# The first four feature units of a hybrid decoder block share each k-step

## Chip, core and metric

The kernel runs on one core of one Trainium2 chip. The metric is device time in microseconds (us) of one execution of the whole program; lower is better. TensorE is called PE, VectorE DVE, ScalarE ACT, GpSimd POOL, and SyncE, which here only issues transfers, SP.

## What is computed

One decoder layer on a sequence of 512 tokens with 1024 channels, everything in float32. Cut to what matters here:

```
h    = rms_norm(x, norm_mix_g)                       # x: (1, 512, 1024)
proj = h @ w_in                                      # 1024 -> 12288 features
glu_in, q, k, v, g, gate_logits = split(proj)
a = glu_in[:, :1024] * sigmoid(glu_in[:, 1024:])     # GLU, then a depthwise conv of 31 taps, layer norm, silu
y_a = a @ w_conv_proj + b
r = retention(rotary(q), rotary(k), v)               # 4 heads, chunks of 128, norm, gate silu(g)
y_b = r @ w_ret_proj
x = x + (sigmoid(gA) * y_a + sigmoid(gB) * y_b) @ w_out
x = x + gated_conv_mlp(rms_norm(x))
return rms_norm(x)
```

## The kernel before

Activations lie with channels on the 128 partitions and the 512 tokens along the free dimension, so a tile of 128 channels is 128x512 and x is eight such tiles (`xs`, one for each step `kt` of a contraction over 1024 channels). The norm's factor of each token is not known when the first products start: x is only scaled by the channel gains (`g0`), multiplied, and the product is multiplied by the factor of its tokens (`rB`) when it is read out of PSUM.

Every float32 product is made of three float32r products. An operand is split into a high part (a cast on ACT) and a low part (original minus high, on DVE): `split_scaled` does it for x (`xg`), `split_half` for weights (`whi`, `wlo`, from the raw `wraw`). A matmul of a feature unit (128 features x 512 tokens in one PSUM bank) is then high x high, high x low, low x high for each of eight k-steps: 24 matmuls of 512 columns.

Weights come as one long stream of "halves" (128x1024, 512 KB, eight blocks of 128x128, so one half is one unit). `load_half` issues the transfer, `split_half` the two casts; `blocks` hands out the next blocks in order and through `upto` makes sure that halves up to `LOOK` = 2 ahead are emitted. Three buffers each hold `wraw`, `whi` and `wlo`.

At the start there is no work that needs less than x. The first two units (`unit_pair`) share each k-step, for which the stream's first two halves are stored interleaved; the third and fourth unit (`unit`) follow one after the other. `SumSq` squares each x tile on ACT and adds the squares on DVE; `stat` sums them over the channels with two matmuls against ones (line 238), DVE picks the result, POOL takes the power, and two small transfers turn it into `rB`. `stat`'s pair `wait` says after how many calls of `tick` (one for a unit) each of its stages is emitted.

The order of instructions on each engine is fixed when the program is built (a scheduler works from priorities; `tc.high_priority` moves some), and each engine then works strictly in its own order. The depthwise conv on DVE (line 368, 240 instructions) has a low priority and fills DVE between other work.

Of the kernel before, what the change touches and what calls it, by code (L numbers as in the profile page):

```python
# [9 lines left out]
F32 = mybir.dt.float32  # L10
F32R = mybir.dt.float32r
AF = mybir.ActivationFunctionType
ALU = mybir.AluOpType

P = 128
S = 512
D = 1024
KT = D // P
# [8 lines left out]
EPS = 1e-6  # L27
HS = 8 * P
LOOK = 2
WARM = 9  # L30
WPRIO = 100


_PC = {}
# [13 lines left out]
def hybrid_block(  # L48
# [10 lines left out]
    nc = tc.nc  # L59
    sb = ctx.enter_context(tc.tile_pool(name="sb", bufs=1))  # L60
# [4 lines left out]
    def nm(s):  # L65
        uid[0] += 1
        return f"{s}_{uid[0]}"

    def t512(tag, bufs, dt=F32):
        return sb.tile([P, S], dt, tag=tag, bufs=bufs, name=nm(tag))  # L70

    def tmp():
        return t512("t", 8)

    def bank():
        return psp.tile([P, S], F32, tag="ps", name=nm("ps"))

    def f32(ap):
        return ap.bitcast(F32)

    par = sb.tile([P, NPARAM], F32, tag="par", name="par")
# [6 lines left out]
    halves = {}  # L88
    emitted = [0]

    raws = {}

    def load_half(h):
        raw = sb.tile([P, HS], F32, tag="wraw", bufs=3, name=nm("wraw"))
        cut = (0, 2 * P, HS) if h == 0 else (0, HS)
        raws[h] = raw, [slice(u, v) for u, v in zip(cut, cut[1:])]
        for sl in raws[h][1]:
            nc.sync.dma_start(out=raw[:, sl], in_=wst[h][:, sl])

    def split_half(h):  # L100
        raw, sls = raws.pop(h)
        hi = sb.tile([P, HS], F32R, tag="whi", bufs=3, name=nm("whi"))
        lo = sb.tile([P, HS], F32R, tag="wlo", bufs=3, name=nm("wlo"))
        with tc.high_priority(offset=WPRIO if h > 1 else 0):
            for sl in sls:
                nc.scalar.copy(out=hi[:, sl], in_=raw[:, sl])  # L106
                nc.vector.tensor_tensor(out=lo[:, sl], in0=raw[:, sl], in1=f32(hi[:, sl]),  # L107
                                        op=ALU.subtract)
        halves[h] = (hi, lo)

    def upto(h):
        while emitted[0] <= min(h, NBLK - 1):
            load_half(emitted[0])
            split_half(emitted[0])
            emitted[0] += 1

    pos = [0]

    def blocks(n):
        b = pos[0]  # L120
        pos[0] += n
        h, c = divmod(b, 8)
        upto(h + LOOK)
        hi, lo = halves[h]
        sl = slice(c * P, (c + n) * P)
        return hi[:, sl], lo[:, sl]
# [3 lines left out]
    def later(n, fn):  # L130
        pending.append([n, fn])

    def tick():
        due = []
        for p in pending:
            p[0] -= 1
            if p[0] == 0:
                due.append(p)
        for p in due:
            pending.remove(p)  # L140
            p[1]()

    def unit(ps, rhs):
        last = len(rhs) - 1
        for kt, (xh, xl) in enumerate(rhs):
            wh, wl = blocks(1)
            nc.tensor.matmul(ps, lhsT=wh, rhs=xh, start=kt == 0, stop=False)  # L147
            nc.tensor.matmul(ps, lhsT=wh, rhs=xl, start=False, stop=False)  # L148
            nc.tensor.matmul(ps, lhsT=wl, rhs=xh, start=False, stop=kt == last)  # L149
        tick()  # L150
        return ps

    def unit_pair(rhs):
        pair = (bank(), bank())
        last = len(rhs) - 1
        for kt, (xh, xl) in enumerate(rhs):
            wh, wl = blocks(2)
            for i, ps in enumerate(pair):
                sl = slice(i * P, (i + 1) * P)
                nc.tensor.matmul(ps, lhsT=wh[:, sl], rhs=xh, start=kt == 0, stop=False)  # L160
                nc.tensor.matmul(ps, lhsT=wh[:, sl], rhs=xl, start=False, stop=False)
                nc.tensor.matmul(ps, lhsT=wl[:, sl], rhs=xh, start=False, stop=kt == last)
        tick()
        tick()
        return pair

    def split(src, tag, bufs):
        h = t512(tag, bufs, F32R)
# [5 lines left out]
    def split_scaled(src, g, tag, bufs):  # L174
        h = t512(tag, bufs, F32R)
        l = t512(tag, bufs, F32R)
        nc.scalar.activation(out=h, in_=src, func=AF.Copy, scale=g)
        nc.vector.scalar_tensor_tensor(
            out=l, in0=src, scalar=g, in1=f32(h), op0=ALU.mult, op1=ALU.subtract)
        return h, l  # L180
# [72 lines left out]
    def rsqrt_eps(v, eps):  # L253
        nc.vector.tensor_scalar(out=v, in0=v, scalar1=eps, scalar2=None, op0=ALU.add)
        return rsqrt(v)

    def stat(ss, n, eps, use, wait, dst):

        run = sums(ss)

        def second():
            ps = run()
            r = rsqrt_eps(pick(ps, n), eps)
            row = dram.tile([P, NCH], F32, tag="row", bufs=2, name=nm("row"))
            nc.gpsimd.dma_start(out=row, in_=r)
            b = t512(dst, 1)
            flat = row.rearrange("p c -> (p c)").rearrange("(o t) -> o t", o=1)
            nc.gpsimd.dma_start(out=b, in_=flat.broadcast_to([P, S]))
            later(wait[1], lambda: use(b, ps))

        later(wait[0], second)
# [8 lines left out]
    warm_ps = bank()  # L280
    for _ in range(WARM):
        nc.tensor.matmul(warm_ps[:, 0:P], lhsT=ones, rhs=ones, start=True, stop=True)
    xs = []
    g0 = sb.tile([P, KT], F32, tag="g0", name="g0")
    for i in range(KT):
        t = t512("x", 8)
        nc.sync.dma_start(out=t, in_=xT[i * P:(i + 1) * P, :])
        xs.append(t)
        if i == 0:
            nc.sync.dma_start(out=g0, in_=params[:, _PC["norm_mix_g"]:_PC["norm_mix_g"] + KT])  # L290
            load_half(0)
        if i == 3:
            load_half(1)
    ident = sb.tile([P, P], F32, tag="ident", name="ident")
    nc.sync.dma_start(out=ident, in_=ident_in)
    nc.sync.dma_start(out=par, in_=params)
    identr = sb.tile([P, P], F32R, tag="identr", name="identr")
    nc.gpsimd.tensor_copy(out=identr, in_=ident)
    onesr = sb.tile([P, P], F32R, tag="onesr", name="onesr")
    nc.gpsimd.tensor_copy(out=onesr, in_=ones)  # L300
    xg = []
    for i in range(KT):
        xg.append(split_scaled(xs[i], g0[:, i:i + 1], "xg", 16))
        if i in (0, 3):
            split_half(emitted[0])
            emitted[0] += 1

    class SumSq:
        def __init__(self):
# [10 lines left out]
    ss = SumSq()  # L320
# [4 lines left out]
    rB = [None]  # L325
# [11 lines left out]
    def times_r(ps):  # L337
        t = tmp()
        nc.vector.tensor_tensor(out=t, in0=ps, in1=rB[0], op=ALU.mult)  # L339
        return t  # L340
# [6 lines left out]
    def glu_units():  # L347
        return times_r(unit(bank(), xg)), times_r(unit(bank(), xg))

    def glu_first():  # L350
        ps = [*unit_pair(xg), unit(bank(), xg), unit(bank(), xg)]
        ts = [times_r(p) for p in ps]
        return ts[:2], ts[2:]

    def glu(ta, sg):
        nc.scalar.activation(out=sg, in_=sg, func=AF.Sigmoid)
# [46 lines left out]
        later(4, centre)  # L403


    def rope():
        p1 = unit(bank(), xg)
        p2 = unit(bank(), xg)
        res = []
        for u, v, op in ((p1, p2, ALU.subtract), (p2, p1, ALU.add)):  # L410
            m1 = tmp()
            m2 = tmp()
            nc.vector.tensor_tensor(out=m1, in0=u, in1=cosr, op=ALU.mult)
            nc.vector.tensor_tensor(out=m2, in0=v, in1=sinr, op=ALU.mult)
            nc.vector.tensor_tensor(out=m1, in0=m1, in1=m2, op=op)
            res.append(split(m1, "A", 16))
        return res
# [96 lines left out]
                add_into(yb[m], ps)  # L514


    stat(ss.acc, D, EPS, norm_mix, (2, 2), "rB")
    rg = None
    for h in range(H):
        ps = [glu_units() for _ in range(2)] if h else glu_first()  # L520
        for i in range(2):
            a = glu(*ps[i])
            with tc.high_priority(offset=-1200):
                conv(2 * h + i, a)
        dec = t512("dec", 1)
        nc.sync.dma_start(out=dec, in_=decay[h])
        q = rope()
        k = rope()
        if rg is not None:
            ret_proj(h - 1, rg)  # L530
        v = values()
        sc = scores(q, k, dec)
        sgs = []
        for e in range(DV // P):
            t = times_r(unit(bank(), xg))
            s_ = t512("G", 4)
            nc.scalar.activation(out=s_, in_=t, func=AF.Silu)
            sgs.append(s_)
        banks = inner(sc, v)
        rg = ret_norm(h, banks, sgs)  # L540
# [8 lines left out]
    for mp in range(KT // 2):  # L549
        sB = [gate(KT + 2 * mp + i, tmp()) for i in range(2)]  # L550
        for i in range(2):
            m = 2 * mp + i
            ps = unit(bank(), rg)
# [3 lines left out]
    for m in range(KT):  # L557
        ps = unit(bank(), cv)
        t = tmp()
# [4 lines left out]
    ss = SumSq()  # L564
    x1 = []
    x1g = []
    for m in range(KT):
        x_ = t512("x", 8)
        nc.sync.dma_start(out=x_, in_=xT[m * P:(m + 1) * P, :])
        ps = unit(bank(), mix)  # L570
# [46 lines left out]
    ss = SumSq()  # L617
# [174 lines left out]
```

## Time and profile before

| | |
|---|---|
| time of the runs (three) | 1086.47 to 1087.11 us, median 1087.07 |
| the profiled execution | 1086.47 us, of which span 1084.7 us |
| PE busy | 1073.2 us (99% of the span), 4834 matmuls |
| DVE / ACT / POOL busy | 71% / 39% / 2% |
| granted TensorE clock | 0.998 of full speed on average |
| read from HBM | 104.41 MB, 98 GB/s over the span |

The span runs from the first to the last instruction; 1.8 us lie around it. A busy share says how long an engine worked, not whether anything waited for it; the waits and the chain of work tell that.

### The profile page before, as it was taken

Reading aid. Unit: us, or ns where it says so; the run is one execution under the profiler, and the core shown is the slowest. Engines: PE = TensorE matmul, PEld = TensorE weight load, DVE = VectorE, ACT = ScalarE, POOL = GpSimd, SP = SyncE. Lnnn points to the kernel's source line nnn. Section 1 sums busy time; section 2 is a strip of 40 time slices with the busy share of each in tenths; the row PEclk is TensorE's granted clock in tenths of the full one; section 3 lists DMA queues with packets and bytes.
Section 4 is the critical chain, followed back from the end, with each engine's and each line's share of the span. In section 5 each row is a group of like instructions: output and inputs, shape, how many; then the busy total and the mean of one; then the engine's idle time right before and its main releaser. Section 6 shows DMA issues by size and latency. Waiting matters only on the chain.

```text
span 1084.7 us, 12428 instructions
## 1 busy us (share of the span) xinstructions
PE 1073.2 (99%) x4834; PEld 883.2 (81%) x4834; DVE 770.0 (71%) x1126; ACT 418.3 (39%) x556; POOL 24.8 (2%) x88
## 2 busy tenths in 40 slices
PE   8999999999999999999999999999999999999996
PEld 6888888888888888888888888888888888888886
DVE  7899899758996699948764555677676236767433
ACT  6334332533234331535542234444443113444331
POOL 1000000000000000000000000000000000000000
PEclk9999999999999999999999999999999999999999
DMA  7223232323322232222323532332222223222212
GB/s 274 91 98 105 68 99 95 107 68 98 98 97 88 72 110 99 81 78 88 107 98 107 146 117 98 88 113 85 94 97 97 97 98 98 90 86 97 98 58 79
DMA packets 33259, 107.33 MB, mean 99 GB/s; under 512 B 3952, under 2 KB 6256, under 8 KB 33200
## 3 DMA queue, kind: packets, MB, share of 16 engines
q1 hardware_dynamic: 32416, 104.69, 29.1%
q0 software_dynamic: 784, 1.85, 1.0%
q8 instruction: 38, 0.62, 0.2%
q14 instruction: 21, 0.17, 0.1%
HBM read 104.41 MB, written 2.11 MB: 98 GB/s over the span
## 4 chain that ended last, share of the span: by engine, by line
PE 97%; issue 1%; DVE 1%; DMA 0%; SPq 0%; POOLq 0%; ACT 0%; POOL 0%; DVEq 0%
PE ps L147 28%; PE ps L149 28%; PE ps L148 28%; PE ps L427 3%; PE ps L426 3%; PE ps L428 3%; PE ps L484 1%; PE ps L485 1%; PE ps L483 1%; PE ps L460 0%; PE ps L462 0%; PE ps L458 0%; DVE ss L183 0%; DMA x<-in_xT_dram 0%; PE ps L238 0%
## 5 line engine op out<-in xcount | busy, mean ns | idle before, releaser
L106 ACT CAST whi<-wraw 128x1024 fp32r<-128x1024 f32 (+1 forms) x185 | 193.2, 1045 | 356.5 <-PE ps L148 258.3
L107 DVE TENSOR_TENSOR wlo<-wraw,whi 128x1024 fp32r<-128x1024 f32 (+1 forms) x185 | 224.7, 1215 | 62.1 <-ACT whi L106 61.9
L147 PE MATMUL ps<-xg,whi 128*128 128x512 f32 x672 | 262.1, 390 | 0.0
L148 PE MATMUL ps<-xg,whi 128*128 128x512 f32 x672 | 261.7, 389 | 0.0
L149 PE MATMUL ps<-xg,wlo 128*128 128x512 f32 x672 | 261.5, 389 | 0.0
L149 PE MATMUL ps<-A,wlo 128*128 128x512 f32 x448 | 176.5, 394 | 0.0
L147 PE MATMUL ps<-A,whi 128*128 128x512 f32 x448 | 176.5, 394 | 0.0
L368 DVE SCALAR_TENSOR_TENSOR C<-ap,par,C 128x512 f32<-128x512 f32 x240 | 166.4, 744 | 2.9 <-ACT C L365 2.6
L148 PE MATMUL ps<-A,whi 128*128 128x512 f32 x384 | 151.3, 394 | 0.0
L149 PEld LDWEIGHTS ps<-xg,wlo 128*128 128x128 f32 x672 | 126.2, 188 | 26.5
L147 PEld LDWEIGHTS ps<-xg,whi 128*128 128x128 f32 x672 | 126.2, 188 | 26.1
L148 PEld LDWEIGHTS ps<-xg,whi 128*128 128x128 f32 x672 | 126.2, 188 | 26.1
L149 PEld LDWEIGHTS ps<-A,wlo 128*128 128x128 f32 x448 | 83.8, 187 | 20.9
L147 PEld LDWEIGHTS ps<-A,whi 128*128 128x128 f32 x448 | 83.8, 187 | 20.7
L148 PEld LDWEIGHTS ps<-A,whi 128*128 128x128 f32 x384 | 71.8, 187 | 17.7
L589 DVE SCALAR_TENSOR_TENSOR t<-ap,par,t 128x512 f32<-128x512 f32 x96 | 71.7, 750 | 2.3 <-ACT t L586 0.7
L339 DVE TENSOR_TENSOR t<-ps,rB 128x512 f32<-128x512 f32 x48 | 32.5, 685 | 55.2 <-PE ps L149 55.2
L183 DVE TENSOR_TENSOR x<-x,ps 128x512 f32<-128x512 f32 (+1 forms) x50 | 33.0, 663 | 53.4 <-PE ps L149 49.9
L583 DVE TENSOR_TENSOR ap<-ps,rB 128x512 f32<-128x512 f32 x48 | 33.1, 691 | 48.4 <-PE ps L149 45.5
L147 PE MATMUL ps<-R,whi 128*128 128x512 f32 x160 | 63.0, 394 | 0.0
L148 PE MATMUL ps<-R,whi 128*128 128x512 f32 x160 | 63.0, 394 | 0.0
L149 PE MATMUL ps<-R,wlo 128*128 128x512 f32 x160 | 63.0, 394 | 0.0
(147 smaller groups left out, 1175.8 us busy)
## 6 DMA issues: line engine op xcount, KB each, us to landing
wraw<-in_wst_dram SPq DMA_DIRECT2D x183, 512.0 KB, 3.3
x<-in_xT_dram SPq DMA_DIRECT2D x16, 256.0 KB, 2.7
out_dram<-t SPq DMA_DIRECT2D x8, 256.0 KB, 2.3
nB<-row POOLq DMA_DIRECT2D x5, 256.0 KB, 4.7
dec<-in_decay_dram SPq DMA_DIRECT2D x4, 256.0 KB, 2.6
t<-in_cs_dram SPq DMA_DIRECT2D x2, 256.0 KB, 4.0
rB<-row POOLq DMA_DIRECT2D x2, 256.0 KB, 4.1
wraw<-in_wst_dram SPq DMA_DIRECT2D x1, 384.0 KB, 3.7
```

Of the source, the lines that this page charges most:

```text
L106: nc.scalar.copy(out=hi[:, sl], in_=raw[:, sl])
L107: nc.vector.tensor_tensor(out=lo[:, sl], in0=raw[:, sl], in1=f32(hi[:, sl]), op=ALU.subtract)
L147: nc.tensor.matmul(ps, lhsT=wh, rhs=xh, start=kt == 0, stop=False)
L148: nc.tensor.matmul(ps, lhsT=wh, rhs=xl, start=False, stop=False)
L149: nc.tensor.matmul(ps, lhsT=wl, rhs=xh, start=False, stop=kt == last)
L183: nc.vector.tensor_tensor(out=acc, in0=acc, in1=v, op=ALU.add)
L368: nc.vector.scalar_tensor_tensor(out=acc, in0=a[:, k:k + S], scalar=wcol(k), in1=acc, op0=ALU.mult, op1=ALU.add)
L426: nc.tensor.matmul(banks[c], lhsT=xh[:, sl], rhs=wh, start=kt == 0, stop=False)
L427: nc.tensor.matmul(banks[c], lhsT=xl[:, sl], rhs=wh, start=False, stop=False)
L428: nc.tensor.matmul(banks[c], lhsT=xh[:, sl], rhs=wl, start=False, stop=kt == KT - 1)
L583: nc.vector.tensor_tensor(out=u[:, FK - 1:], in0=ps, in1=rB[0], op=ALU.mult)
L589: nc.vector.scalar_tensor_tensor(out=c, in0=u[:, k:k + S], scalar=wcol(k), in1=c, op0=ALU.mult, op1=ALU.add)
```

## The change

The first four units now share each k-step (`unit_quad`): at each k-step four matmuls high x high, four with the low part of x, four with the low part of the weights, into four banks. The sums of squares (`stat` with wait (1, 2)) are emitted after k-step `QSUM` = 5, inside the quad. The unit that follows the four (the first of q) is emitted before their results are read out.

Halves 0 and 1 (the interleaved pair) go into `raw01`, halves 2 and 3 into four 128x512 tiles `raw23`, and their high and low parts into eight tiles with the name R (`side`). All four are fetched in pieces: the pair in pieces of one k-step (128x256), one more, and then two k-steps each; each side half in pieces of 2, 2 and 4 k-steps. Pieces are split as they come, by `cut`; the very first piece's high part is made on DVE (`tensor_copy`), not on ACT. The gains `g0` and the first piece of the pair are issued from ACT's queue, everything else from SP's.

```diff
+QSUM = 5
...
-    def unit_pair(rhs):
-        pair = (bank(), bank())
...
+    def unit_quad(rhs):
+
+        quad = [bank() for _ in range(4)]
         last = len(rhs) - 1
         for kt, (xh, xl) in enumerate(rhs):
-            wh, wl = blocks(2)
...
+            h, c = divmod(kt, 4)
+            ws = [tuple(w[:, (2 * c + i) * P:(2 * c + i + 1) * P] for w in halves[h])
+                  for i in range(2)]
+            ws += [tuple(w[:, c * P:(c + 1) * P] for w in side[i][h]) for i in range(2)]
+            for p in range(3):
+                for ps, (wh, wl) in zip(quad, ws):
+                    nc.tensor.matmul(ps, lhsT=wl if p == 2 else wh, rhs=xl if p == 1 else xh,
+                                     start=kt == 0 and p == 0, stop=kt == last and p == 2)
+            if kt in (3, 4):
+                upto(kt + 1)
+            if kt in (QSUM, last):
+                tick()
...
+    load_x(0)
+    load_pair(0, 1, nc.scalar)
+    load_side(0, 2)
+    load_x(1)
+    load_pair(1, 1)
+    load_x(2)
+    load_pair(2, 2)
+    load_side(2, 2)
+    load_x(3)
+    load_x(4)
+    load_pair(4, 2)
+    load_side(4, 4)
+    load_x(5)
+    load_x(6)
+    load_pair(6, 2)
+    load_x(7)
+    emitted[0] = 4
...
+    for k in range(KT):
+        if k == 0:
+            split_pair(0, 1, nc.vector.tensor_copy)
+        if k == 1:
+            split_pair(1, 1)
+        xg.append(split_scaled(xs[k], g0[:, k:k + 1], "xg", 16))
+        if k == 0:
+            split_side(0, 2)
...
-        ps = [*unit_pair(xg), unit(bank(), xg), unit(bank(), xg)]
+        ps = unit_quad(xg)
+        q1 = unit(bank(), xg)
...
-    stat(ss.acc, D, EPS, norm_mix, (2, 2), "rB")
+    stat(ss.acc, D, EPS, norm_mix, (1, 2), "rB")
```

SP's queue at the start of the program, before (x is a tile of x, g the gains, wraw a raw weight half):

```order
L287 DMA x_81<-in_xT_dram 128x512
L290 DMA g_80<-in_params_dram 128x8
L98 DMA wraw_84<-in_wst_dram 128x256
L98 DMA wraw_84<-in_wst_dram 128x768
L287 DMA x_87<-in_xT_dram 128x512
```

and of the change (G are the raw tiles of the side halves):

```order
L301 DMA x_82<-in_xT_dram 128x512
L311 DMA G_92<-in_wst_dram 128x256
L311 DMA G_94<-in_wst_dram 128x256
L301 DMA x_83<-in_xT_dram 128x512
L306 DMA wraw_90<-in_wst_dram 128x256
L301 DMA x_84<-in_xT_dram 128x512
L306 DMA wraw_90<-in_wst_dram 128x512
```

The gains and the first piece of the pair have gone to ACT's queue. That queue at the start, with the change:

```order
L292 DMA g_80<-in_params_dram 128x8
L287 ACT_TABLE_LOAD
L287 COPY tok_68<-neghalf 128x4
L306 DMA wraw_90<-in_wst_dram 128x256
L185 ACTIVATE xg_131<-x_82,g_80 128x512
```

The first piece's transfer stands behind the table load and a small copy. DVE's queue at the start, before:

```order
L178 SCALAR_TENSOR_TENSOR xg_111<-x_81,g_80,xg_110 128x512
L107 TENSOR_TENSOR wlo_115<-wraw_84,whi_114 128x256
L107 TENSOR_TENSOR wlo_115<-wraw_84,whi_114 128x768
L178 SCALAR_TENSOR_TENSOR xg_121<-x_87,g_80,xg_120 128x512
L183 TENSOR_TENSOR ss_152<-ss_152,t_154 128x512
```

and of the change, to where the second x tile comes:

```order
L186 SCALAR_TENSOR_TENSOR xg_132<-x_82,g_80,xg_131 128x512
L101 TENSOR_TENSOR R_97<-G_92,R_96 128x256
L100 CAST whi_104<-wraw_90 128x256
L101 TENSOR_TENSOR R_101<-G_94,R_100 128x256
L101 TENSOR_TENSOR wlo_105<-wraw_90,whi_104 128x256
L186 SCALAR_TENSOR_TENSOR xg_142<-x_83,g_80,xg_141 128x512
```

The cast that the first matmul reads (whi_104) is DVE's third instruction. DVE a little later with the change, where the last squares are added and the sums' low part (t_215) is made:

```order
L186 SCALAR_TENSOR_TENSOR xg_180<-x_89,g_80,xg_179 128x512
L191 TENSOR_TENSOR ss_188<-ss_188,t_208 128x512
L101 TENSOR_TENSOR wlo_273<-wraw_270,whi_272 128x1024
L241 TENSOR_TENSOR t_215<-ss_188,t_214 128x512
L101 TENSOR_TENSOR wlo_291<-wraw_288,whi_290 128x1024
```

Between the last addition and t_215 stands the low part of one whole half, that of the unit after the quad. PE at that place, with the change:

```order
L166 MATMUL ps_220<-xg_169,R_99 128x512
L166 MATMUL ps_221<-xg_169,R_103 128x512
L246 MATMUL ps_306<-t_214,onesr 128x512
L246 MATMUL ps_306<-t_215,onesr 128x512
L166 MATMUL ps_218<-xg_175,whi_106 128x512
```

Both matmuls of the sums stand after k-step 5, with k-steps 6 and 7 behind them. Before, the first stood after the pair and the second six matmuls into the third unit.

## Rows read from the trace of the kernel before

**Rows 1.** The page: its span, and the chain that ended last by engine.
```profile
span 1084.7 us, 12428 instructions
...
PE 97%; issue 1%; DVE 1%; DMA 0%; SPq 0%; POOLq 0%; ACT 0%; POOL 0%; DVEq 0%
```

**Rows 2.** Waits of PE: line, releaser: us in total, times, longest.
```profile
PE ps L222 <- DVE tokr L215: 1.2, 1, 1.2
...
PE ps L191 <- ACT t L643: 1.0, 1, 1.0
PE ps L160 <- ACT xg L177: 0.9, 1, 0.9
```

**Rows 3.** Timeline of PE: start us, us, what (times merged), idle before and releaser.
```profile
5.03 0.73 PE L160 MATMUL ps<-xg,whi 128*128 128x512 f32 x2 [0.23 <-ACT whi L106]
...
13.95 0.40 PE L161 MATMUL ps<-xg,whi 128*128 128x512 f32 x1
...
18.27 0.39 PE L162 MATMUL ps<-xg,wlo 128*128 128x512 f32 x1
...
20.65 0.50 PE L238 MATMUL ps<-t,onesr 128*128 128x512 f32 x1 [0.27 <-DVE t L233]
...
30.54 0.39 PE L147 MATMUL ps<-xg,whi 128*128 128x512 f32 x1
```

**Rows 4.** Timeline of ACT at the start.
```profile
0.73 1.28 ACT L279 ACT_TABLE_LOAD   x1 [0.73 <-PEq L782]
2.03 0.19 ACT L279 COPY tok<-neghalf 128x4 f32<-128x4 f32 x1
3.44 0.63 ACT L314 ACTIVATE ss<-x 128x512 f32<-128x512 f32 x1 [1.22 <-DMA x<-in_xT_dram]
3.97 0.71 ACT L177 ACTIVATE xg<-x,g 128x512 fp32r<-128x512 f32 x1
```

**Rows 5.** Timeline of DVE, to the first use of rB.
```profile
4.71 0.75 DVE L178 SCALAR_TENSOR_TENSOR xg<-x,g,xg 128x512 fp32r<-128x512 f32 x1 [4.71 <-ACT xg L177]
5.38 0.42 DVE L107 TENSOR_TENSOR wlo<-wraw,whi 128x256 fp32r<-128x256 f32 x1
6.70 0.96 DVE L107 TENSOR_TENSOR wlo<-wraw,whi 128x768 fp32r<-128x768 f32 x1 [0.91 <-ACT whi L106]
...
17.64 2.34 DVE L107 TENSOR_TENSOR wlo<-wraw,whi 128x1024 fp32r<-128x1024 f32 x2
...
19.92 0.68 DVE L233 TENSOR_TENSOR t<-ss,t 128x512 fp32r<-128x512 f32 x1
...
32.00 0.69 DVE L335 TENSOR_TENSOR cosr<-t,rB 128x512 f32<-128x512 f32 x1 [4.22 <-DMA rB<-row]
```

**Rows 6.** First issue on SP, and transfers issued up to 2.8 us: KB, us to landing.
```profile
0.74 0.40 SPq L287 DMA_DIRECT2D x<-in_xT_dram  x1
...
x<-in_xT_dram SPq DMA_DIRECT2D x1, 256.0 KB, 2.7
g<-in_params_dram SPq DMA_DIRECT2D x1, 4.0 KB, 2.4
wraw<-in_wst_dram SPq DMA_DIRECT2D x1, 128.0 KB, 2.6
x<-in_xT_dram SPq DMA_DIRECT2D x1, 256.0 KB, 4.2
```

**Rows 7.** GB/s moved in each us from 0 to 40.
```profile
GB/s 0 49 227 232 294 319 352 424 391 406 403 408 429 422 406 401 160 0 0 37 242 381 328 238 393 402 84 21 33 205 418 131 0 0 0 0 0 152 365 8
```

**Rows 8.** DVE's busy time from 40 to 110 us, a copy, and both sides of head 0's sums.
```profile
40.00:110.00 70.00, 70.00 (x331) 59.12 (x331) 70.00 (x107) 26.78 (x41) 0.12 (x1) 1.00 0.28 95
...
107.93 0.41 DVE L373 COPY ss<-C 128x512 f32<-128x512 f32 x1
...
114.70 0.68 DVE L233 TENSOR_TENSOR t<-ss,t 128x512 fp32r<-128x512 f32 x1
...
118.27 0.61 PE L238 MATMUL ps<-t,onesr 128*128 128x512 f32 x2
```

More of the change, by code (lines that the diff above doesn't have):

```diff
@@ L94, in load_half, with cut, pair_tiles @@
         raw = sb.tile([P, HS], F32, tag="wraw", bufs=3, name=nm("wraw"))
[L95 to L98, printed above, removed]
-    def split_half(h):
[L101 to L109, printed above, removed]
+        nc.sync.dma_start(out=raw, in_=wst[h])
+        raws[h] = raw
+    def cut(hi, lo, raw, sl=slice(0, HS), eng=None):
+        (eng or nc.scalar.copy)(out=hi[:, sl], in_=raw[:, sl])
+        nc.vector.tensor_tensor(out=lo[:, sl], in0=raw[:, sl], in1=f32(hi[:, sl]),
+                                op=ALU.subtract)
+    def pair_tiles():
+        return (sb.tile([P, HS], F32R, tag="whi", bufs=3, name=nm("whi")),
+                sb.tile([P, HS], F32R, tag="wlo", bufs=3, name=nm("wlo")))
+    def split_half(h):
+        halves[h] = pair_tiles()
+        with tc.high_priority(offset=WPRIO):
+            cut(*halves[h], raws.pop(h))
     def upto(h):
@@ L151, in unit @@
         return ps
-    def unit_pair(rhs):
-        pair = (bank(), bank())
+    def unit_quad(rhs):
+        quad = [bank() for _ in range(4)]
         last = len(rhs) - 1
         for kt, (xh, xl) in enumerate(rhs):
-            wh, wl = blocks(2)
[L158 to L165, printed above, removed]
+            h, c = divmod(kt, 4)
[10 more added lines that the diff above has]
+                tick()
+        pos[0] += 4 * len(rhs)
+        return quad
     def split(src, tag, bufs):
@@ L282, in hybrid_block @@
         nc.tensor.matmul(warm_ps[:, 0:P], lhsT=ones, rhs=ones, start=True, stop=True)
-    xs = []
     g0 = sb.tile([P, KT], F32, tag="g0", name="g0")
[L285 to L293, printed above, removed]
-    ident = sb.tile([P, P], F32, tag="ident", name="ident")
+    nc.scalar.dma_start(out=g0, in_=params[:, _PC["norm_mix_g"]:_PC["norm_mix_g"] + KT])
@@ new lines, in hybrid_block, with load_x, load_pair @@
+    xs = [t512("x", 8) for _ in range(KT)]
+    raw01 = [sb.tile([P, HS], F32, tag="wraw", bufs=3, name=nm("wraw")) for _ in range(2)]
+    raw23 = [[t512("G", 4) for _ in range(2)] for _ in range(2)]
+    side = [[(t512("R", 8, F32R), t512("R", 8, F32R)) for _ in range(2)] for _ in range(2)]
+    for h in range(2):
+        halves[h] = pair_tiles()
+    def load_x(k):
+        nc.sync.dma_start(out=xs[k], in_=xT[k * P:(k + 1) * P, :])
+    def load_pair(k, n, eng=nc.sync):
+        h, c = divmod(k, 4)
+        sl = slice(2 * c * P, 2 * (c + n) * P)
+        eng.dma_start(out=raw01[h][:, sl], in_=wst[h][:, sl])
@@ new lines, in load_side, with split_pair, split_side @@
+    def load_side(k, n, eng=nc.sync):
+        h, c = divmod(k, 4)
+        for i in range(2):
+            eng.dma_start(out=raw23[i][h][:, c * P:(c + n) * P],
+                          in_=wst[2 + i][:, k * P:(k + n) * P])
+    def split_pair(k, n, eng=None):
+        h, c = divmod(k, 4)
+        cut(*halves[h], raw01[h], slice(2 * c * P, 2 * (c + n) * P), eng)
+    def split_side(k, n):
+        h, c = divmod(k, 4)
+        for i in range(2):
+            cut(*side[i][h], raw23[i][h], slice(c * P, (c + n) * P))
@@ new lines, in hybrid_block @@
+    load_x(0)
[15 more added lines that the diff above has]
+    emitted[0] = 4
+    ident = sb.tile([P, P], F32, tag="ident", name="ident")
+    identr = sb.tile([P, P], F32R, tag="identr", name="identr")
+    xg = []
+    for k in range(KT):
[6 more added lines that the diff above has]
+            split_side(0, 2)
+        if k == 1:
+            split_pair(2, 2)
+            split_side(2, 2)
+        if k == 3:
+            split_pair(4, 2)
+            split_side(4, 4)
+        if k == 5:
+            split_pair(6, 2)
@@ L295, in hybrid_block @@
     nc.sync.dma_start(out=ident, in_=ident_in)
-    nc.sync.dma_start(out=par, in_=params)
-    identr = sb.tile([P, P], F32R, tag="identr", name="identr")
     nc.gpsimd.tensor_copy(out=identr, in_=ident)
@@ L300, in hybrid_block @@
     nc.gpsimd.tensor_copy(out=onesr, in_=ones)
[L301 to L306, printed above, removed]
+    nc.sync.dma_start(out=par, in_=params)
     class SumSq:
@@ L350, in glu_first @@
     def glu_first():
-        ps = [*unit_pair(xg), unit(bank(), xg), unit(bank(), xg)]
+        ps = unit_quad(xg)
+        q1 = unit(bank(), xg)
         ts = [times_r(p) for p in ps]
-        return ts[:2], ts[2:]
+        return (ts[:2], ts[2:]), q1
     def glu(ta, sg):
@@ L403, in conv_norm, with rope @@
         later(4, centre)
-    def rope():
-        p1 = unit(bank(), xg)
+    def rope(p1=None):
+        p1 = p1 or unit(bank(), xg)
         p2 = unit(bank(), xg)
@@ L514, in ret_proj @@
                 add_into(yb[m], ps)
-    stat(ss.acc, D, EPS, norm_mix, (2, 2), "rB")
+    stat(ss.acc, D, EPS, norm_mix, (1, 2), "rB")
     rg = None
     for h in range(H):
-        ps = [glu_units() for _ in range(2)] if h else glu_first()
+        ps, q1 = ([glu_units() for _ in range(2)], None) if h else glu_first()
         for i in range(2):
@@ L526, in hybrid_block @@
         nc.sync.dma_start(out=dec, in_=decay[h])
-        q = rope()
+        q = rope(q1)
         k = rope()
```

## Prediction

> **What bounds the kernel now.** I read the page first: the chain of work that ended last is PE for 97% of a span of 1084.7 us [rows 1]. PE's matmuls follow one another with nothing between, so only what PE does not do in its own rhythm can be won. The list of waits says where that is: two waits late in the program (1.2 and 1.0 us, lines 222 and 191, which the change does not touch), and otherwise waits in the first 21 us, the longest of 0.9 us for a tile of x [rows 2]. Then I read the timeline of PE there. From 13.95 to 18.27 us it starts 20 matmuls, 19 steps of 0.2274 us: this is its rhythm. From the first product at 5.03 us to the first matmul of unit five at 30.54 us it starts 98 (four units of 24, two for the sums) [rows 3]. In rhythm these take 98 x 0.2274 = 22.28 us; they took 25.51. So **3.2 us** are lost between 5.03 and 30.54 us, and that is all this change can reach, plus or minus a shift of the first product.
>
> Why they are lost shows on the side of the suppliers. The pair consumes a k-step of 384 KB (256 of x, 128 of weights) in 6 matmuls, 1.36 us, which is 288 GB/s. Transfers move 230 to 320 GB/s between 2 and 6 us and 350 to 430 after that [rows 7], and DVE, which makes every low part and adds the squares, is the engine that the sums' second matmul waits for at 20.65 us [rows 3].
>
> **The change, step by step.** *The rhythm needed.* A k-step of the quad is 12 matmuls, 2.73 us, on 256 KB of x and 256 KB of weights: 192 GB/s instead of 288. The eight x tiles, which are most of the work of ACT and DVE, are spread over 21.8 us of PE's work instead of 10.9. That is what can remove the 3.2 us; the next four steps ask what comes in their place.
>
> *The first product.* Before it starts at 5.03 us. With the change it needs DVE's third instruction. x lands at 3.44 us [rows 4]; ACT's high part takes 0.71 [rows 4], DVE's low part 0.75 [rows 5], the first side piece's low part 0.42 as that of 256 columns did [rows 5], less about 0.07 of overlap at each step as in these rows: 5.25 us. Then the cast of the first weight piece, which no row shows on DVE: a 512-column copy on DVE took 0.41 [rows 8], so 0.2 to 0.4 and I take 0.3. That gives 5.6 us as the earliest start. But the piece must be there. ACT issues it after the gains' transfer, the table load and the copy: 0.74 + 0.40 (an issue on SP [rows 6]; no row shows one on ACT, and I take between nothing and twice this) + 1.28 + 0.19 [rows 4] = 2.6 us. Bounds of its landing: 2.4 to 2.6 us after issue, as 4 KB and 128 KB took [rows 6], is 5.0 to 5.2; if it lines up behind all bytes issued before it on both queues (768 KB) it lands near the x tile that had 768 KB ahead and landed 4.2 us after its issue near 2.6 us [rows 6], at 6.8. I take 5.6, nearer to the lower end, because the row of the same size is the nearer one and that also had a 256 KB tile ahead of it. The first product then starts at 5.6 + 0.3 + 0.05 = **5.95 us**, which costs 0.92 us (0.6 to 2.1).
>
> *The k-steps after it.* PE needs k-step 1 at 5.95 + 2.73 = 8.7 us; its x tile lands by about 6 to 6.8, and two tile splits take 1.5 us. Each later k-step gives ACT and DVE 2.73 us for one x tile (split, square, add: about 1.3 us on either) and 512 columns of weights (0.6). I put stalls there at nothing; the cover is about 1 us per k-step.
>
> *The sums inside the quad.* They stand after k-step 5, so PE comes to the first at 5.95 + 72 x 0.2274 = 22.3 us and to the second at 22.55. DVE must by then have done what it did before from 4.71 to 20.60 us (15.9 us, of which 0.9 idle [rows 5]), plus the low part of one more whole half that stands ahead of the sums' low part (1.17, half of 2.34 [rows 5]), the cast (0.3), and six more, smaller pieces (0.1 each, from 0.42 us for 256 columns against 1.17 for 1024 [rows 5]), with perhaps 0.4 idle for pieces at the start. From 4.2 us that is 4.2 + 15.0 + 1.2 + 0.3 + 0.6 + 0.4 = 21.7 us. 0.9 us of cover is left: nothing, but this is the thinnest place. What is queued behind these two matmuls is all of k-steps 6 and 7.
>
> *What is late next.* rB. The second sum moves from 20.65 to 22.55 us, and DVE picks it up without the half it did in between (0.5 us), so rB comes at about 33.4 instead of 32.0 us [rows 5]. PE does not wait for rB directly (it has three more units and free banks), but DVE does. From 40 to 110 us DVE has no idle time at all [rows 8], and it ends this stretch with the low part of head 0's sums at 114.70 + 0.68 = 115.4 us, which PE reads 0.23 us after 118.27, that is 3.1 us later [rows 8]. With the change PE comes there 2.3 us earlier and DVE 1.4 later less one half's low part, which now stands before the wait for rB (1.1): 0.5 us of cover is left. I put this at nothing too.
>
> *Everything else.* The borrowed tiles (names G and R) and the four banks are needed again only in head 0's later stages, after rB has long been used; more issues on SP (18 for 12 up to the last x tile) cost 0.40 us each [rows 6] for 128 to 256 KB, faster than these bytes flow. These edits I put at nothing. The sum is 3.2 - 0.92 = **2.3 us** less. Against the profiled execution (1086.47) this is 1084.2; it was the fastest of the three runs, so against the median of 1087.07 I forecast **1084.8 us** (0.21% less).
>
> The Trainium skill, "DMA: Bandwidth & Descriptors", section "Measured (HBM→SBUF, 128 partitions, SWDGE, issued from GpSimd)", speaks against small pieces: at least 1 MiB for 75% of peak, 138 GB/s at 64 KB. The trace differs for this queue: x tiles of 256 KB flow at about 400 GB/s when several are under way [rows 7]; pieces of 128 KB one after another no row shows. By the page's 64 KB rate (an estimate from that page) the 5.0 MB of rival C below would take until 38 us and the kernel about 1103 us; by the row it is the sum above.
>
> **Rivals.**
> *A, as summed*: a start at 5.6 to 6.2 us and no other wait: 1084.3 to 1085.1 us. Chance 0.58; the line of 0.2% runs through it.
> *B, the first piece is late.* It lines up behind what SP issued, lands at 6.3 to 6.8, PE starts at 6.7 to 7.2 and the gain is 1.0 to 1.5 us: 1085.8. For it: the table load ahead of it and one stream of bytes. Against: it is small, and the nearest row took 2.6 us. Chance 0.18.
> The Trainium skill says on that page, "Issuing engines are not separate DMA queues", that a second issuing engine saves only issue time; no transfer of this trace comes from ACT, so no run here shows it yet.
> *C, slower.* The small pieces slow the stream, and the wait moves to the sums. Everything up to the half whose low part stands before the sums (x, five halves, the parameters) is 5.0 MB, flowing from about 2 us. At 400 GB/s it is in by about 16 us; at 230, the rate of 2 to 4 us [rows 7], by 23.7. With about 1.2 us for its cast on ACT (an estimate, under twice the 0.71 of rows 4), 1.2 and 0.7 on DVE the second sum starts near 26.8 instead of 22.55: 4.2 us lost, 1.9 more than the gain, 1089.0. It decides from there: 0.2% slower needs a stream that stays at or below about 230 GB/s up to 20 us; the gain is gone at about 250. For it: six pieces of 128 KB and eighteen issues. Against: 350 to 430 GB/s in rows 7 with tiles of 256 KB. Chance 0.12, half of it beyond 0.2%.
> *D, given back in head 0.* The 0.5 us of cover at head 0's sums is not there, since rB comes later or DVE's filler runs longer: each us that DVE is late PE waits. With 1.5 us more on DVE 1.0 us of the gain goes: 1085.8. For it: 70 of 70 us busy. Against: DVE has the same list of work less one half. Chance 0.12.
>
> **Numbers.** What a measurement here can tell from no change is 0.2%, 2.2 us. Faster by more: 0.47 of A and 0.02 of D, 0.49. Within: 0.11 of A, 0.17 of B, 0.10 of D, 0.06 of C, 0.44. Slower: 0.01 of B and 0.06 of C, 0.07. The range goes from the earliest start and a little (1084.2) to B and D with their larger prices (1086.4); outside are most of C and the ends of B and D.
>
> **What would show it.** Right: PE's first product between 5.6 and 6.2 us, waiting for a DVE cast; the 98 matmuls without another wait, so that unit five starts near 28.2 instead of 30.54; rB used near 33.4; head 0's sums near 116 us without a wait. Wrong: a first product after 6.5 us (B), idle PE before the sums inside the quad (C), a wait of PE for DVE near 116 us (D).

## The result, and the profile after

| | before | with the change |
|---|---|---|
| median of the timed runs | 1087.09 us (1086.47 to 1087.72) | 1080.49 us (1080.33 to 1080.83) |
| the profiled execution | 1086.47 us, span 1084.7 | 1080.83 us, span 1079.0 |

The ratio is 0.994, with an interval of 0.9922 to 0.9957: **6.6 us faster**, where the forecast was 2.3 us and its range ended at 1084.2. The page, then PE's timeline at the places of [rows 3] and [rows 8] (columns as there):

```profile
span 1079.0 us, 12449 instructions
...
PE 1069.1 (99%) x4834; PEld 884.3 (82%) x4834; DVE 770.4 (71%) x1133; ACT 417.7 (39%) x561; POOL 26.0 (2%) x88
```

```profile
5.90 0.70 PE L166 MATMUL ps<-xg,whi 128*128 128x512 f32 x2 [0.69 <-DVE whi L100]
6.43 1.03 PE L166 MATMUL ps<-xg,R 128*128 128x512 f32 x2
...
22.73 0.61 PE L246 MATMUL ps<-t,onesr 128*128 128x512 f32 x2
...
28.62 0.39 PE L149 MATMUL ps<-xg,whi 128*128 128x512 f32 x1
...
116.35 0.62 PE L246 MATMUL ps<-t,onesr 128*128 128x512 f32 x2
```

The part of the program that the forecast spoke of went nearly as it said. The first product starts at 5.90 us (forecast 5.95), unit five at 28.62 (28.2), head 0's sums at 116.35 (116) without a wait. Unit five is 1.92 us earlier than in [rows 3]. So 3.7 us of the 5.6 between the two profiled executions (3.8 of the 5.7 between their spans) lie behind it, where both kernels run the same matmuls and PE has the same two waits (1.2 and 1.0 us).

They are in PE's rhythm. The first head's retention output moves R tiles in 96 matmuls that follow one another without a wait; here is their first and last, before the change and then with it:

```profile
151.36 0.39 PE L147 MATMUL ps<-R,whi 128*128 128x512 f32 x1
...
173.53 0.39 PE L149 MATMUL ps<-R,wlo 128*128 128x512 f32 x1
```

```profile
149.44 0.39 PE L149 MATMUL ps<-R,whi 128*128 128x512 f32 x1
...
170.98 0.39 PE L151 MATMUL ps<-R,wlo 128*128 128x512 f32 x1
```

95 steps in 22.17 us are 233.4 ns each, in 21.54 us 226.7. The program has 480 matmuls of 512 columns that move R tiles, and 480 x 6.7 ns = 3.2 us. Nothing about these matmuls is in the diff. What it does change is where R's tiles lie: `side` takes R's eight buffers at the start of the program, and the pool lays names out in the order in which they are first used. In the built program R's first tile starts at byte 212672 of each partition before and at 56320 with the change, that is 192 and 0 past a multiple of 512. The weight tiles start on multiples of 512 in both.

A second rhythm like that of R before is still there with the change. In the FFN's first products, which move A tiles, the first and the last of 471 matmuls:

```profile
690.22 0.39 PE L150 MATMUL ps<-A,whi 128*128 128x512 f32 x1
...
799.88 0.39 PE L149 MATMUL ps<-A,whi 128*128 128x512 f32 x1
```

109.66 us over 470 steps: 233.3 ns. A starts 448 past a multiple of 512, before and after.

### The profile page after: what moved, and what is told of

Same layout as the page of the kernel before. It is cut to its first block, busy times and chain, and to the rows that moved or that the text cites. A ratio compares the mean times of both kernels' runs of the same rounds, so it can differ in the third digit from the quotient of the medians.

```text
span 1079.0 us, 12449 instructions
## 1 busy us (share of the span) xinstructions
PE 1069.1 (99%) x4834; PEld 884.3 (82%) x4834; DVE 770.4 (71%) x1133; ACT 417.7 (39%) x561; POOL 26.0 (2%) x88
## 4 chain that ended last, share of the span: by engine, by line
PE 98%; issue 1%; DMA 0%; DVE 0%; SPq 0%; POOLq 0%; POOL 0%; DVEq 0%; ACT 0%
PE ps L149 27%; PE ps L151 27%; PE ps L150 27%; PE ps L486 3%; PE ps L484 3%; PE ps L485 3%; PE ps L166 2%; PE ps L542 1%; PE ps L543 1%; PE ps L541 1%; PE ps L518 0%; PE ps L520 0%; PE ps L516 0%; DMA G<-in_wst_dram 0%; PE ps L246 0%
## 5 line engine op out<-in xcount | busy, mean ns | idle before, releaser
L100 ACT CAST whi<-wraw 128x1024 fp32r<-128x1024 f32 (+2 forms) x184 | 191.3, 1040 | 330.0 <-PE ps L150 235.4
L101 DVE TENSOR_TENSOR wlo<-wraw,whi 128x1024 fp32r<-128x1024 f32 (+2 forms) x185 | 222.6, 1203 | 61.2 <-ACT whi L100 61.2
L149 PE MATMUL ps<-xg,whi 128*128 128x512 f32 x656 | 255.8, 390 | 0.0
L150 PE MATMUL ps<-xg,whi 128*128 128x512 f32 x656 | 255.3, 389 | 0.0
L151 PE MATMUL ps<-xg,wlo 128*128 128x512 f32 x656 | 255.3, 389 | 0.0
L151 PEld LDWEIGHTS ps<-xg,wlo 128*128 128x128 f32 x656 | 123.1, 188 | 25.8
L150 PEld LDWEIGHTS ps<-xg,whi 128*128 128x128 f32 x656 | 123.2, 188 | 25.5
L149 PEld LDWEIGHTS ps<-xg,whi 128*128 128x128 f32 x656 | 123.2, 188 | 25.3
```

Source lines behind the costliest of these rows:

```text
L100: (eng or nc.scalar.copy)(out=hi[:, sl], in_=raw[:, sl])
```

## The experiments

**Theory P**: besides the order, the change moved R, and a matmul's step depends on where its moving tile starts. **Rival S**: order and pieces made all of it. All edits below add only 64-byte (or 32-byte) tiles that nothing reads, or move one line, unless said otherwise; each added tile is also cleared once by POOL, in a line that the diffs leave out. Starts of tiles are those of the built programs.

**e1: the change, R put 64 bytes off.**
```diff
+    pad0 = sb.tile([P, 16], F32, tag="pad0", name="pad0")
     side = [[(t512("R", 8, F32R), t512("R", 8, F32R)) for _ in range(2)] for _ in range(2)]
+    pad1 = sb.tile([P, 16], F32, tag="pad1", name="pad1")
```


> The changed kernel with its whole schedule, but R's eight tiles start 64 bytes later (56384, which is 64 past a multiple of 128, as R's tiles stood in the kernel before), while whi, wlo and xg stay on multiples of 128. Theory P (placement: a 512-column matmul step takes 226.7 ns where the moving tile starts on a multiple of 128 and 233.3 ns where it starts 64 past one): the 480 steps that move R tiles take 6.7 ns more each, 3.2 us, so 1083.7, and the 512-column steps on R are back at 233. Rival S (the new order and the split pieces alone made the gain of 6.6 us, the place of a tile is nothing): 1080.5, as the changed kernel.

Measured: 1084.58 us (1084.38 to 1086.75; ratio 0.9979, 0.997 to 0.9989). The same 96 matmuls:
```profile
151.61 0.39 PE L149 MATMUL ps<-R,whi 128*128 128x512 f32 x1
...
173.77 0.39 PE L151 MATMUL ps<-R,wlo 128*128 128x512 f32 x1
```
233.3 ns. S falls: with the whole schedule in place, 64 bytes take 4.1 us back, somewhat more than the 3.2 expected. Three of its ten runs lie 2 us above the others, the profiled one among them; what its profile shows of that comes with e8.

**e2: the kernel before, 64 bytes ahead of R and nothing else.**
```diff
         def use(rs, _):
+            if h == 0:
+                pad = sb.tile([P, 16], F32, tag="pad0", name="pad0")
```


> The kernel before with nothing of the change, but 64 bytes are left free ahead of R's first tile, so that R starts at 212736, a multiple of 128, in place of 212672. Theory P: 480 steps by 6.7 ns less, 3.2 us, so 1083.9 against 1087.1. Rival S: 1087.1, no change.

Measured: 1083.35 us (1083.11 to 1083.83; ratio 0.9962, 0.9948 to 0.9977), 4.2 us below the runs of before beside it (the two profiled executions, 1086.47 and 1083.27, differ by 3.2).
```profile
151.62 0.39 PE L147 MATMUL ps<-R,whi 128*128 128x512 f32 x1
...
173.16 0.39 PE L149 MATMUL ps<-R,wlo 128*128 128x512 f32 x1
```
226.7 ns. Without any of the change, between half and two thirds of its gain is there.

**e3: the change, 64 bytes ahead of C** (A lies behind C and moves with it).
```diff
+        if i == 0:
+            pad = sb.tile([P, 16], F32, tag="pad0", name="pad0")
         acc = t512("C", 8)
```


> The changed kernel with 64 bytes left free ahead of C's first tile, so that C and A (and sh and sl behind them) start on multiples of 128 in place of 64 past one. Theory P: the 1418 steps on C and A tiles that take 233.3 ns in the changed kernel take 226.7, 9.5 us less, so 1071.0. Rival S: 1080.5, no change. A third way, that only tiles in the first part of the memory are fast (R moved from 212672 to 56320, too): also 1080.5, with the steps on A still at 233.

Measured: 1071.85 us (1070.77 to 1072.69; ratio 0.9853, 0.9836 to 0.9869). The steps on A are 226.7 ns (485 steps in 109.94 us). The third way falls too: A lies at 183808, in the upper part of the memory, and is fast.

**e5: the change, 32 bytes ahead of C** (the same edit with 8 columns).

> The changed kernel with 32 bytes left free ahead of C, so that C and A start 96 past a multiple of 128 (in place of 64 past one). It asks how the price depends on the offset. If any offset costs the same 6.7 ns: 1080.5. If the price is in proportion to the bytes past the multiple (10 ns at 96): 1418 steps by 3.3 ns more, 1085.2. If it is in proportion to the bytes up to the next multiple (3.3 ns at 96): 1075.8. Rival S, where the place is nothing: 1080.5 too, which the run with 64 bytes must tell apart.

Measured: 1081.56 us (1080.47 to 1082.41; ratio 0.9945, 0.993 to 0.996), the steps on A 233.3 ns. The price isn't in proportion to the offset.

**e6: the kernel before, 64 bytes ahead of C**, which puts R right as well.

> The kernel before with nothing of the change, and 64 bytes left free ahead of C's first tile: C, A, sh, sl and R all start on multiples of 128. It is to be set beside the changed kernel with the same 64 bytes (1071.85 in the last runs), so that what is left between them is the order and the pieces alone. Theory P (placement and order add up): the steps on R, C and A, about 1900 of 233.3 ns, take 6.7 ns less each, 12.7 us off 1087.1 to 1087.6, so 1074.4 to 1074.9, and the order's own part is 2.5 to 3.1. Rival (the order's part is what the forecast summed, 2.3, or less since the first products sometimes run at half rate): the same 1074.4, but the changed kernel no more than 2.3 below it in the median.

Measured: 1074.07 us (1073.9 to 1074.83; ratio 0.988, 0.9866 to 0.9895). It stands 2.2 us above e3 and, below, 2.9 above e13: **what order and pieces are worth by themselves.** More closely it isn't known, and the rival (no more than 2.3) is not ruled out: unit five starts at 31.09 us in e6's profile, at 30.00 in e3's and at 28.18 in e13's, by how the start went (see e8). Placement alone is worth 13 us in the kernel before.

**e7: the change, whi and wlo 64 bytes off**; **e12: the change, xg 64 bytes off** (in both a tile of 64 bytes ahead of the name and one behind, so that all that is allocated later moves by 128). In e7 the weights start 64 past a multiple of 512, xg 128, A 64 and R 0; in e12 the weights start at 0, xg at 64, A at 64 and R at 0.

> The changed kernel with the weight tiles whi and wlo started 64 bytes past a multiple of 128, and R and xg left on multiples. The weights are mostly the stationary operand; in the 384 steps of the values they are the moving one. Theory P for the moving operand alone: 384 steps by 6.7 ns, 2.6 us, 1083.1. Rival, that the stationary tile's place counts as well: some 4400 steps by up to 6.7 ns, 29 us more, 1110. Rival, that only xg, A, C and R matter for another reason than their start: 1080.5.

> The changed kernel with xg's sixteen tiles started 64 bytes past a multiple of 128 (98368) and everything else as it stood, C and A 64 past one as in the changed kernel. Some 1890 of its 512-column steps move xg tiles at 226.7 ns. Theory P: they take 233.3, 12.6 us more, 1093.1, slower than the kernel before, whose order it does not have. Rival (the two step times belong to something else of R, C and A): 1080.5.

Measured: e7 1084.59 us (1084.32 to 1086.73; ratio 0.9978, 0.9968 to 0.9987), e12 1082.57 (1082.52 to 1084.19; ratio 0.996, 0.9945 to 0.9975). Neither fits P. In e12 the steps on xg did not go to 233.3, and in e7 those on A, which still start 64 past a multiple of 128, became fast. xg (two stretches) and A in e7, then xg and A in e12:
```profile
28.64 0.39 PE L149 MATMUL ps<-xg,whi 128*128 128x512 f32 x1
...
50.38 0.39 PE L151 MATMUL ps<-xg,wlo 128*128 128x512 f32 x1
...
123.33 0.40 PE L151 MATMUL ps<-xg,wlo 128*128 128x512 f32 x1
...
151.33 0.40 PE L151 MATMUL ps<-xg,wlo 128*128 128x512 f32 x1
...
690.13 0.39 PE L151 MATMUL ps<-A,wlo 128*128 128x512 f32 x1
...
799.83 0.39 PE L149 MATMUL ps<-A,whi 128*128 128x512 f32 x1
```
```profile
122.98 0.39 PE L151 MATMUL ps<-xg,wlo 128*128 128x512 f32 x1
...
150.45 0.39 PE L151 MATMUL ps<-xg,wlo 128*128 128x512 f32 x1
...
690.03 0.39 PE L151 MATMUL ps<-A,wlo 128*128 128x512 f32 x1
...
799.90 0.39 PE L151 MATMUL ps<-A,wlo 128*128 128x512 f32 x1
```
96 and 121 matmuls on xg and 485 on A in e7 (228.8, 233.3 and 226.7 ns), 121 and 481 in e12 (228.9 and 228.9). So I formed rule Q: what counts is the difference between the starts of the moving tile and the weight tile.

**e13: the change, every tile that PE reads 64 bytes off**; **e14: the change with rtok's 64 bytes allocated earlier.**
```diff
+    pad1 = sb.tile([P, 16], F32, tag="pad1", name="pad1")
     xs = [t512("x", 8) for _ in range(KT)]
...
+            pad = sb.tile([P, 16], F32, tag="pad0", name="pad0")
         acc = t512("C", 8)
```
```diff
+    r_tok = sb.tile([P, 4 * NCH], F32, tag="rtok", name="rtok")[:, 0:NCH]
     side = [[(t512("R", 8, F32R), t512("R", 8, F32R)) for _ in range(2)] for _ in range(2)]
...
-    r_tok = sb.tile([P, 4 * NCH], F32, tag="rtok", name="rtok")[:, 0:NCH]
```


> The changed kernel with 64 bytes left free ahead of C and 64 more ahead of the x tiles: every tile that TensorE reads (R, whi, wlo, xg, onesr, t, C, A) starts 64 past a multiple of 128, and moving and weight tiles differ by multiples of 128. Rule P (the moving tile's own start): all 4280 steps at 233.3, 28 us more than the run with only C's 64 bytes, 1100. Rule Q (the difference of the starts of the moving and the weight tile; a multiple of 128 is free): 1071 to 1072.7, as in that run.

> The changed kernel with one line moved and no bytes added: the 64 bytes of rtok, which lie between the weight tiles and C, are allocated ahead of R. R, whi, wlo and xg move up by 64; C and A stay exactly where they are in the changed kernel (183744, 64 past a multiple of 128), so that only their difference to the weights changes, from 448 to 384 past a multiple of 512. Rule P: the steps on C and A stay at 233, and those on R, xg and the moving weights join them, 2750 by 6.7 ns: 1099. Rule Q with a period of 128: the steps on C and A fall to 226.7, 9.5 us less: 1071.0, the same as with the 64 bytes ahead of C. Rule Q with a period of 256, in which 128 is as bad as 64: 1080.5.

Measured: e13 1071.16 us (1070.9 to 1071.79; ratio 0.9854, 0.9839 to 0.9869), e14 1081.88 (1080.44 to 1082.19; ratio 0.9948, 0.9931 to 0.9965). A in e13, then in e14:
```profile
690.00 0.39 PE L149 MATMUL ps<-A,whi 128*128 128x512 f32 x1
...
799.94 0.39 PE L151 MATMUL ps<-A,wlo 128*128 128x512 f32 x1
```
```profile
690.20 0.40 PE L150 MATMUL ps<-A,whi 128*128 128x512 f32 x1
...
799.88 0.39 PE L151 MATMUL ps<-A,wlo 128*128 128x512 f32 x1
```
485 steps of 226.7 ns in e13: a tile's own start is nothing, and P in its first form is gone by 29 us. 472 steps of 232.4 ns in e14, while R, xg and the moving weights, all shifted with the weight tiles, stay at 226.7: Q holds, but with a period above 128. Put together, each cell is the mean over a stretch of one moving tile (first to last start; starts are taken modulo 512):

| moving minus weight tile | where | ns a step |
|---|---|---|
| 0 | xg before and after; R after; A in e3, e6, e7 and e13 | 226.7 |
| 256 | R in e2 and e6 | 226.7 |
| 64 | xg and A in e12; xg in e7 | 228.9; 228.8 and 233.3 |
| 192 | R before | 233.4 |
| 384 | A in e14 | 232.4 |
| 448 | A before and after; R in e1 and e7; the values' weights in e7 and e12 | 233.3 to 233.4 |
| 480 | A in e5 | 233.3 |

The difference alone does not fix the step. At 64, the same xg tiles over weight tiles with the same start took both values within e7. And at 0, R in e12 took 227.2 ns over its first 96 matmuls: behind those on xg its first ten steps lay between 224 and 236 ns, the later ones at 226.7. A in e14, at 384, took 233.3 in a later stretch (889.84 to 1001.60 us).

**e8, e10, e11: the start.** The runs of one kernel with one placement differed by 2 us, and the profiles show where. In e1's profiled execution (1086.75 us) and in that of e10:
```profile
5.98 1.19 PE L166 MATMUL ps<-xg,whi 128*128 128x512 f32 x2 [0.78 <-DVE whi L100]
...
8.68 1.06 PE L166 MATMUL ps<-xg,R 128*128 128x512 f32 x2
9.53 1.06 PE L166 MATMUL ps<-xg,wlo 128*128 128x512 f32 x2
10.38 0.67 PE L166 MATMUL ps<-xg,R 128*128 128x512 f32 x2
10.89 0.62 PE L166 MATMUL ps<-xg,whi 128*128 128x512 f32 x2
```
```profile
0.99 2.50 PE L290 MATMUL ps<-ones 128*128 128x128 f32 x10 [0.99 <-POOL neghalf L285]
5.86 1.19 PE L166 MATMUL ps<-xg,whi 128*128 128x512 f32 x2 [2.36 <-ACT R L100]
...
8.56 1.05 PE L166 MATMUL ps<-xg,R 128*128 128x512 f32 x2
9.41 0.96 PE L166 MATMUL ps<-xg,wlo 128*128 128x512 f32 x2
10.21 0.63 PE L166 MATMUL ps<-xg,R 128*128 128x512 f32 x2
```
Two steps take 0.85 us until about 10 us, then 0.46: the lower of the clock's two levels (1.2 GHz), then the higher (2.4 GHz), though the granted clock in the profile's rows stands at 1.00 all through. The Trainium skill, "TensorE: Matmul & The Clock Gate", section "Wait — 56ns, not 53.3ns?", gives 426.7 ns a step of 512 columns at the lower level, and these rows agree with 0.427; for the higher it gives 215.7, and no stretch of such steps in this kernel, at 226.7 and more, shows that. In the profile of the change the steps were at full rate from 6.2 us on. The idle stretch ahead of the first product does not decide it alone: with the same nine warm-up products at the lower level and 0.67 to 0.78 us of idle time, the profiles of e7, e12 and e13 show full rate there too, those of e1, e3 and e14 half rate. e8 and e11 are e3 with `WARM` = 11 and 13, e10 with 5, in place of 9.

> The changed kernel with C aligned (1071.85; single runs at 1070.8 to 1071.1 and at 1072.7) and 11 warm-up products in place of 9. In the profile of that kernel the warm-up ended at 5.2, the first product began at 5.95, and its first products ran at half rate, 0.43 us a step, until 9.4; in the changed kernel's own profile they ran at 0.23 from 6.2 on. Theory G (the idle stretch of 0.75 us ahead of the first product is what delays the rise): with it filled to 5.85 no execution shows half-rate products past 7, all runs lie at 1070.8 to 1071.1, median down by 0.5 to 1. Rival (when the clock rises is chance, the gap has no part in it): both kinds of run stay, and the median is 1071.9 or more.

> The changed kernel with C aligned (1071.85; single runs from 1070.8 to 1072.7) and 5 warm-up products in place of 9, so that the warm-up ends at 3.3 and TensorE idles 2.7 us ahead of its first product. Theory G (what TensorE did ahead of the first product decides how long its first products run at half rate): half-rate steps of 0.43 us in the profile until 9 or later, in nearly every execution, so a median of 1072.5 to 1074. Rival (chance): the same mix as with 9, a median of 1071 to 1072.

> The same with 13 warm-up products: at half rate they end at 6.7, 0.7 us past the time at which the first product could start, and at full rate from about 4.8 on they end near 5.8. Theory G: no half-rate products behind the warm-up in any run; single runs from 1070.6 to 1071.6 and none at 1072.7, as with 11 (1070.85). Rival (chance): 1072 or more in a part of the runs, and the 0.7 us lost in these.

Measured: e8 1070.85 us (1070.57 to 1071.59; ratio 0.9851, 0.9836 to 0.9865), the lowest of all; e10 1072.89 (1072.78 to 1073.38; ratio 0.9869, 0.9852 to 0.9885); e11 1072.08 (1071.4 to 1072.9; ratio 0.986, 0.9845 to 0.9875). e10 fits theory G: its profile and the times of all four runs look as if they paid (at e3's two in four, chance would give that once in 16, an estimate). e8 fits it nearly (one run, 1071.59, lies above the 1071.1 that was expected), but is no proof: its clock had already risen at 4.8 us, ahead of the products that were added, and e13 with 9 had no run above 1071.8 either. e11 lost for another reason, the next one.

**e9: e3 with the first weight cast on ACT.**
```diff
-    load_pair(0, 1, nc.scalar)
+    load_pair(0, 1)
...
-            split_pair(0, 1, nc.vector.tensor_copy)
+            split_pair(0, 1)
```


> The changed kernel with C aligned, and the first pair's piece fetched by SP right behind the first x tile and rounded on ScalarE, behind the first xg, in place of on VectorE, where it stood behind two other operations (it began at 5.5 with its piece landed by 4.4). Theory: the first product starts at about 4.9 in place of 5.95, inside the warm-up, so there is no idle stretch; the side pieces and the second x tile are issued 0.45 later, so the second k-step begins near 8.3 in place of 8.6: 0.3 us off the 1070.8 of the runs whose first products ran at full rate, and none at 1072.7. Rival: the later second x tile and side pieces take it back or more: 1071.2 to 1072.

Measured: 1072.05 us (1071.61 to 1073.34; ratio 0.9862, 0.9848 to 0.9877). The first product did start at 4.85 and the second k-step at 7.99 (8.68 in e13), so the rival's late second tile is not what took the gain back. PE and DVE at head 0's sums read:
```profile
115.78 0.50 PE L246 MATMUL ps<-t,onesr 128*128 128x512 f32 x1 [0.33 <-ACT t L240]
116.87 0.50 PE L246 MATMUL ps<-t,onesr 128*128 128x512 f32 x1 [0.58 <-DVE t L241]
```
```profile
114.97 1.25 DVE L101 TENSOR_TENSOR wlo<-wraw,whi 128x1024 fp32r<-128x1024 f32 x1
116.10 0.71 DVE L241 TENSOR_TENSOR t<-ss,t 128x512 fp32r<-128x512 f32 x1
```
With the change these two kinds of DVE instruction stand the other way round:
```profile
115.37 0.69 DVE L241 TENSOR_TENSOR t<-ss,t 128x512 fp32r<-128x512 f32 x1
...
116.58 1.22 DVE L101 TENSOR_TENSOR wlo<-wraw,whi 128x1024 fp32r<-128x1024 f32 x1
```
This is the place of rival D of the prediction, but not its reasons: rB was used at 33.33 us, earlier than with the change (34.08). The built order of e9 puts a half's low part (1.25 us) ahead of the sums' low part, and 0.9 us go in waits. e11's order does so too, and the same two waits are 0.5 and 0.6 us, although PE was ready for the sums at 116.29 us, later than it came to them in e8 (115.96), where it did not wait. Why the program was built in this order in e9 and e11 stays open.

## Why the prediction was wrong, step by step

**The step that failed** is the bound: "3.2 us are lost between 5.03 and 30.54 us, and that is all this change can reach", with its partner "the borrowed tiles (names G and R) ... these edits I put at nothing". I took PE's rhythm, 0.2274 us, from one stage (it moves xg) and held it for all, so a matmul could not become faster. The trace of before showed the second rhythm, 233.4 ns on R between 151.36 and 173.53 us; I had read no rows there. The change takes R's buffers earlier and so moves R from 192 to 0 past a multiple of 512. That term is 480 x 6.7 ns = 3.2 us by the rows; e2 measured 4.2 (by its interval 2.5 to 5.7). With the order's 2.2 to 2.9 the sum is 5.4 to 7.1, and 6.6 was measured. Behind unit five the two spans differ by 3.8 us: 3.2 are these steps, 0.2 steps on xg, and 0.4 lie behind the last matmul.

**The order's own part** was forecast at 2.3 us, and e6 against e3 and e13 gives 2.2 and 2.9. It is a sum that came out for partly wrong reasons:

*The first product*, 5.90 for 5.95, did not wait for its transfer; the number was right by luck. ACT and DVE at the start:
```profile
0.74 0.41 ACTq L292 DMA_DIRECT2D g<-in_params_dram  x1
1.18 1.28 ACT L287 ACT_TABLE_LOAD   x1 [1.18 <-PEq L840]
1.24 0.40 ACTq L306 DMA_DIRECT2D wraw<-in_wst_dram  x1
...
3.71 0.72 ACT L185 ACTIVATE xg<-x,g 128x512 fp32r<-128x512 f32 x1 [1.04 <-DMA g<-in_params_dram]
...
6.50 0.41 ACT L100 CAST R<-G 128x256 fp32r<-128x256 f32 x1 [1.25 <-DMA G<-in_wst_dram]
```
```profile
4.46 0.75 DVE L186 SCALAR_TENSOR_TENSOR xg<-x,g,xg 128x512 fp32r<-128x512 f32 x1 [4.46 <-ACT xg L185]
5.13 0.42 DVE L101 TENSOR_TENSOR R<-G,R 128x256 fp32r<-128x256 f32 x1
5.46 0.29 DVE L100 CAST whi<-wraw 128x256 fp32r<-128x256 f32 x1
...
34.08 0.69 DVE L392 TENSOR_TENSOR cosr<-t,rB 128x512 f32<-128x512 f32 x1 [4.26 <-DMA rB<-row]
```
The piece is issued at 1.24, during the table load and not behind it as I had put it, and landed 3.2 us later, at 4.4, so rival B fell. Its cast waited for DVE's two instructions ahead of it, and these for ACT's xg, which began at 3.71, when the gains had landed, and not with x at 3.44. e9 took the cast off DVE and the product started at 4.85.

*The k-steps*: 0.44 us beyond the rhythm (28.62 - 5.90 - 98 x 0.2274), where nothing was summed. Most is the second side piece, which landed at 6.5 us and holds R's cast up: the pair of matmuls from 6.43 is 0.4 us longer than the pairs behind it. In e13 no pair is longer so, and unit five starts at 28.18, as forecast.

*The sums in the quad* came at 22.73 (forecast 22.3) with no wait, rB was used at 34.08 (33.4), and at head 0's sums DVE's low part ended at 115.37 + 0.69 = 116.06, 0.5 us ahead of the second matmul: the cover was forecast at 0.5, but by two errors that cancel (PE came 1.9 us earlier instead of 2.3, DVE 0.7 later instead of 0.3). That it is thin is what e9 and e11 show, where one half's low part ahead of it is not covered.

*Rival C* and the estimate of 1103 us by the Trainium skill's rate for 64 KB ("DMA: Bandwidth & Descriptors", section "Measured (HBM→SBUF, 128 partitions, SWDGE, issued from GpSimd)") fell together. GB/s in each us from 0, against [rows 7]:
```profile
GB/s 0 43 239 313 236 130 333 383 348 325 315 279 270 361 408 395 420 434 336 147 315 354 324 309 221 262 279 189 1 0 25 168 332 254 8 0 0 0 0 0
```
Pieces of 128 and 256 KB moved 270 to 434 GB/s from 6 to 18 us, far above the 138 that the Trainium skill gives there; the measurement decides for this queue.

## What to carry to other kernels

A rhythm is a term, not a constant: read the step between matmuls in each stage and for each moving tile, and ask why two stages differ. A change that allocates buffers earlier moves every tile behind them, so compare the tables of addresses before calling it free; here 64 bytes are worth 3 to 13 us. An edit at the start can change the built order a hundred microseconds on: read it again where DVE only just delivers, for e9 and e11 lost about 1 us there.

## What was not expected of the hardware

A float32r matmul step of 512 columns settles at 226.7 ns where the starts of the moving and the weight tile differ by 0 or 256 modulo 512, and took 228.8 to 233.4 at the five other differences that were run. Why it is so, why 64 costs 2.2 ns in e12 and in one stretch of e7 and 6.6 in another, and what 128 and 320 do, stays open. The kernel that ran fastest is the change with 64 bytes ahead of C and eleven warm-up products, 1070.85 us, 1.5% below the kernel before; e13, at 1071.16, is not told from it.
